# Allocating the buffers that TensorE reads first, each row on a multiple of 512 bytes

## The chip, the cores and the metric

The kernel runs on one core of a Trainium2 chip. A core has TensorE (PE in the profile; PEld is its loading of stationary operands), VectorE (DVE), ScalarE (ACT), GpSimd (POOL) and SyncE (SP, which here issues DMAs). The engines read their operands from SBUF, which has 128 partitions; a buffer takes the same range of byte addresses in each partition, so a buffer's place is one number, the address within a partition. TensorE writes its results to PSUM.

The metric is the time of one launch on the device, in microseconds (us), as the median of several runs. A profiled execution is one more launch, in which every instruction's start and duration is recorded.

## The reference, cut to what matters

Two sequences of 512 rows and 1024 channels go through the same trunk of two layers, and then a final RMSNorm. In each layer the normalised input is multiplied by one wide matrix; four attention mixers use its columns, each is gated and projected, and the merged sum goes through an output projection that is added to the input:

```python
def _layer(x, ...):
    xn = _rms_norm(x, norm_g)
    h = xn @ w_in
    h_a, h_b, h_c, h_d, z, mg = _split_cols(h, [A_IN, B_IN, C_IN, D_IN, GATE_IN, MERGE_IN])
    ys = [_mla_mixer(h_a, ...), _axial_gqa_mixer(h_b, ...), _sink_window_mixer(h_c, ...), _dilated_mixer(h_d, ...)]
    merged = jnp.zeros_like(x)
    for i in range(N_BRANCH):
        yi = ys[i] * jax.nn.silu(z[..., i * BRANCH_W:(i + 1) * BRANCH_W])
        gi = jax.nn.sigmoid(mg[..., i * D_MODEL:(i + 1) * D_MODEL])
        merged = merged + gi * (yi @ w_branch[i])
    return x + merged @ w_out
```

## The kernel before, in words

Everything is held with channels on the 128 partitions and the 512 rows of a sequence along the free dimension. The program makes four passes, layer by layer and within a layer sequence by sequence; each pass runs a list of steps (projections, attention heads, gates, merges), then the output projection, and prepares the next pass's normalised input. A scheduler of the tile framework sets the order of the instructions on each engine and puts in the semaphores.

**Products in three matmuls.** A float32 operand is split into a high part of type float32r and the rest, its low part. `mm3` (lines 121 to 124) makes one product from three matmuls: high weights by high data (L122), high weights by low data (L123), low weights by high data (L124). Each is 128x128 weights by 128x512 data. A matmul has a moving operand, which is streamed through the array column by column, and a stationary operand, the weights, which PEld loads ahead.

**The buffers that TensorE reads.** `xn0` to `xn7` hold the normalised input of a pass, high and low part as `[P, 2, 512]`; they are the moving operand of the wide projection (`project`, L126, and L656). `y` holds a gated mixer output in two parts, moving operand of the branch projections. `qk` holds queries, keys, latents and the merged sum, as moving and, for keys, as stationary operand. `ph` holds the two parts of the softmax weights (moving), `v` the values (stationary). `wh` and `wl` hold weight tiles of up to 640 columns, high and low part (stationary), made in `piece` (L99) from a tile `wr` that SP loads from DRAM: ScalarE copies the high part (L110), VectorE subtracts (L115), or the low part comes by DMA. Near the end of the last pass four of the `xn` buffers hold weight tiles of the output projection (`kept`), because their data is no longer needed.

**Where buffers lie.** All SBUF buffers come from one pool through `new(tag, shape, dt, bufs)`. A tag's buffers get their place where the tag is first asked for, one after the other from address 16,512 on; later requests for the tag turn over the same buffers. So the order of first requests is the order of addresses. In the kernel before this begins with the small constants (`ident`, `vecs`, `ones`, `heads`), goes on with the first pass's tiles, and a few tags of 64 or 240 bytes in between shift all that follows. A row of a `[P, 2, 512]` buffer is 4096 bytes, its two halves 2048 bytes each. The built program has these places (the last column is the address of the first buffer modulo 512; all buffers of the tag have the same):

| buffers | first to last start, before | modulo 512 |
|---|---|---|
| `s` (2 of 8192 bytes), `wr` (3 of 2560) | 18,432 to 39,936 | 0 |
| `wh`, `wl` (4 of 2560 each) | 42,496 to 60,416 | 0 |
| `qk` (8 of 4096) | 62,976 to 91,648 | 0 |
| `xn0` to `xn7` (4096 each) | 118,656 to 147,328 | 384 |
| `v` (4 of 2048) | 161,280 to 167,424 | 0 |
| `ph` (6 of 2048) | 187,904 to 198,144 | 0 |
| `y` (3 of 4096) | 200,320 to 208,512 | 128 |

Of the kernel before, what the change touches and what calls it, by code (L numbers as in the profile page):

```python
# [7 lines left out]
F32 = mybir.dt.float32  # L8
F32R = mybir.dt.float32r
# [4 lines left out]
P = 128  # L14
T = 512
DM = 1024
NK = DM // P
# [11 lines left out]
def trunk(ctx, tc, x0, x1, wp, wr, wu, wg, wb, wm, wo, vec, rope, msk, eye, y0, y1):  # L29
# [9 lines left out]
    def new(tag, shape, dt=F32, bufs=1):  # L39
        uid[0] += 1  # L40
        return sb.tile(shape, dt, tag=tag, name=f"{tag}_{uid[0]}", bufs=bufs)

    def bank(tag, bufs):
        uid[0] += 1
        return pp.tile([P, T], F32, tag=tag, name=f"{tag}_{uid[0]}", bufs=bufs)
# [15 lines left out]


    ident = new("ident", [P, P])
    vecs = new("vecs", [P, vec.shape[1]])

    def vcol(l, j):
        c = l * 24 + j
        return vecs[:, c : c + 1]

    ones = new("ones", [P, P])  # L70
    nc.vector.memset(ones, 1.0)
    heads = new("heads", [P, P])
# [462 lines left out]
    def begin(xin):  # L535

        nc.scalar.dma_start(out=vecs, in_=vec)
        warm = new("ms", [P, 16], F32, 2)
        act(out=warm, in_=ones[:, 0:16], func=AF.Exp)
        src = wp[0, T_D + 6 * 1]  # L540
        early = [new("s", [P, 4 * T], F32, 2) for _ in range(2)]
        xt = [early[k // 4][:, (k % 4) * T : (k % 4 + 1) * T] for k in range(NK)]
        xg, pieces, acc = [], [], None
        for k in range(NK):
            nc.sync.dma_start(out=xt[k], in_=xin[:, k, :])
            if k % 4 == 0:
                pieces.append(piece(src[k // 4], 512))
            x = new("qk", [P, 2, T], F32R, 8)
            act(out=x[:, 0, :], in_=xt[k], func=AF.Copy, scale=vcol(0, k))
            stt(out=x[:, 1, :], in0=xt[k], scalar=vcol(0, k), in1=f(x[:, 0, :]), op0=ALU.mult, op1=ALU.subtract)  # L550
            xg.append(x)
            acc = squares(acc, xt[k], k)
        load_tabs(("cos", "sin"))
        bc = rstd([acc], ones, DM, "lr")
        ct, st = new("u", [P, T], F32, 2), new("u", [P, T], F32, 2)
        xn = normalise(0, xt, bc, True)
        tt(out=ct, in0=tabs["cos"], in1=bc, op=ALU.mult)
        tt(out=st, in0=tabs["sin"], in1=bc, op=ALU.mult)
        return xn, (xg, pieces, ct, st, bc)
# [283 lines left out]
    xn, early = begin(x0)  # L843
    for n, args in enumerate(passes):
# [4 lines left out]
        xn = layer(*args, xn, ahead, early)  # L849
# [137 lines left out]
```

## Time and profile before

| | |
|---|---|
| median of 3 runs | 2187.64 us (2186.35 to 2188.82) |
| profiled execution, its own time | 2186.45 us |
| span from its first to its last instruction | 2184.7 us |
| granted TensorE clock, mean | 0.985 |
| TensorE matmuls | busy 2120.6 us (97%), 9550 |
| TensorE weight loads | busy 1722.1 us (79%), 9550 |
| VectorE | busy 1795.1 us (82%), 3113 |
| ScalarE | busy 1280.7 us (59%), 2167 |
| GpSimd | busy 411.2 us (19%), 145 |

A row of the groups names the line, the engine, the operation, the written and the read tiles (out<-in), the shape, the count, the busy time and the mean duration. A matmul's recorded duration includes its way through the array, and the next one starts before it ends; so consecutive matmuls are compared by the distance of their starts, which the timeline shows (start, duration, instruction, in us). In the rows of windows the first number is the window's length, then each engine's busy time with the count of instructions in brackets, the granted clock as a share of full speed, the DMA engines' busy share and GB/s.

### The profile page before, as it was taken

Reading aid. Unit: us, or ns where it says so; the run is one execution under the profiler, and the core shown is the slowest. Engines: PE = TensorE matmul, PEld = TensorE weight load, DVE = VectorE, ACT = ScalarE, POOL = GpSimd, SP = SyncE. Lnnn points to the kernel's source line nnn. Section 1 sums busy time; section 2 is a strip of 40 time slices with the busy share of each in tenths; the row PEclk is TensorE's granted clock in tenths of the full one; section 3 lists DMA queues with packets and bytes.
Section 4 is the critical chain, followed back from the end, with each engine's and each line's share of the span. In section 5 each row is a group of like instructions: output and inputs, shape, how many; then the busy total and the mean of one; then the engine's idle time right before and its main releaser. Section 6 shows DMA issues by size and latency. Waiting matters only on the chain.

```text
span 2184.7 us, 28862 instructions
## 1 busy us (share of the span) xinstructions
PE 2120.6 (97%) x9550; PEld 1722.1 (79%) x9550; DVE 1795.1 (82%) x3113; ACT 1280.7 (59%) x2167; POOL 411.2 (19%) x145
## 2 busy tenths in 40 slices
PE   7999999999999999999999998999899999999998
PEld 5887778878888778888888776888688887788887
DVE  8999999987478998785379999999866889997725
ACT  6746675444565767553366466754456757675434
POOL 0032313220013221220002222122200232122200
PEclk9999999999999999999999999999899999999999
DMA  6543444556754445556754434455466544455565
GB/s 213 169 145 120 141 141 163 175 186 210 240 165 145 139 138 159 162 191 212 245 179 155 139 117 134 156 166 177 161 226 223 152 152 135 145 158 164 179 207 185
DMA packets 189798, 369.76 MB, mean 169 GB/s; under 512 B 21328, under 2 KB 30032, under 8 KB 188880
## 3 DMA queue, kind: packets, MB, share of 16 engines
q1 hardware_dynamic: 181152, 351.11, 50.0%
q10 hardware_dynamic: 8496, 16.81, 2.3%
q8 instruction: 75, 1.23, 0.2%
q14 instruction: 75, 0.61, 0.1%
HBM read 273.99 MB, written 93.85 MB: 168 GB/s over the span
## 4 chain that ended last, share of the span: by engine, by line
PE 88%; DVE 8%; issue 1%; DMA 1%; ACT 1%; SPq 0%; DVEq 0%; ACTq 0%
PE mm L122 26%; PE mm L123 26%; PE mm L124 25%; PE so L343 1%; PE so L342 1%; PE ss L351 1%; DVE ph L140 1%; PE ss L352 1%; DMA s<-x 1%; DVE wl L115 1%; PE mi L268 1%; PE ss L124 1%; PE ss L123 1%; PE ss L447 1%; PE ss L122 1%
## 5 line engine op out<-in xcount | busy, mean ns | idle before, releaser
L123 PE MATMUL mm<-xn,wh 128*128 128x512 f32 x1992 | 788.5, 396 | 5.9 <-DVE xn L524 5.9
L122 PE MATMUL mm<-xn,wh 128*128 128x512 f32 x1992 | 791.3, 397 | 1.4 <-ACT xn L523 1.0
L124 PE MATMUL mm<-xn,wl 128*128 128x512 f32 x1992 | 788.7, 396 | 0.0
L110 ACT CAST wh<-wr 128x512 fp32r<-128x512 f32 (+1 forms) x596 | 387.1, 651 | 412.5 <-PE mm L123 302.0
L123 PEld LDWEIGHTS mm<-xn,wh 128*128 128x128 f32 x1992 | 376.3, 189 | 90.7 <-DVE xn L524 6.2
L122 PEld LDWEIGHTS mm<-xn,wh 128*128 128x128 f32 x1992 | 376.0, 189 | 88.8 <-ACT xn L523 1.4
L124 PEld LDWEIGHTS mm<-xn,wl 128*128 128x128 f32 x1992 | 376.1, 189 | 85.8 <-issue 1.0
L291 POOL PARTITION_ALL_REDUCE mr<-mr x64 | 239.2, 3737 | 512.2 <-DVE mr L347 265.8
L286 POOL PARTITION_ALL_REDUCE mr<-mr x64 | 129.8, 2029 | 985.3 <-DVE mr L470 577.5
L115 DVE TENSOR_TENSOR wl<-wr,wh 128x512 fp32r<-128x512 f32 (+2 forms) x304 | 247.2, 815 | 40.2 <-ACT wh L110 36.5
L140 DVE TENSOR_TENSOR ph<-s,ph 128x512 fp32r<-128x512 f32 (+2 forms) x256 | 184.9, 729 | 18.6 <-ACT ph L139 10.3
L139 ACT CAST ph<-s 128x512 fp32r<-128x512 f32 (+2 forms) x256 | 144.8, 577 | 30.6 <-PE so L490 11.0
L210 ACT COPY rs<-mm 32x512 f32<-32x512 f32 x240 | 138.8, 578 | 24.5 <-DVE rx L205 19.2
L713 DVE SCALAR_TENSOR_TENSOR th<-th,mm 128x512 f32<-128x512 f32 x96 | 65.4, 681 | 85.7 <-PE mm L124 83.5
L712 ACT ACTIVATE th<-mm 128x512 f32<-128x512 f32 x96 | 57.5, 599 | 132.2 <-PE mm L124 122.6
L122 PE MATMUL mm<-y,wh 128*128 128x512 f32 x256 | 105.1, 414 | 25.1 <-DVE mg L735 13.7
L122 PE MATMUL mm<-qk,wh 128*128 128x512 f32 (+1 forms) x328 | 122.4, 378 | 6.7 <-ACT wh L110 6.2
L124 PE MATMUL mm<-qk,wl 128*128 128x512 f32 (+1 forms) x328 | 122.3, 376 | 0.5 <-DVE wl L115 0.5
L123 PE MATMUL mm<-qk,wh 128*128 128x512 f32 (+1 forms) x328 | 122.3, 376 | 0.3 <-DVE qk L550 0.3
L124 PE MATMUL mm<-y,wl 128*128 128x512 f32 x256 | 104.4, 408 | 0.0
L123 PE MATMUL mm<-y,wh 128*128 128x512 f32 x256 | 104.1, 407 | 0.0
L327 ACT ACTIVATE s<-ss 128x512 f32<-128x512 f32 x128 | 72.3, 597 | 41.0 <-DVE ph L140 22.3
(182 smaller groups left out, 3247.3 us busy)
## 6 DMA issues: line engine op xcount, KB each, us to landing
wr<-wp SPq DMA_DIRECT2D x248, 256.0 KB, 2.8
wr<-wm SPq DMA_DIRECT2D x192, 320.0 KB, 3.2
lo_wp<-wl SPq DMA_DIRECT2D x124, 256.0 KB, 2.0
wl<-lo_wp SPq DMA_DIRECT2D x124, 256.0 KB, 2.7
lo_wm<-wl SPq DMA_DIRECT2D x96, 320.0 KB, 2.2
wl<-lo_wm SPq DMA_DIRECT2D x96, 320.0 KB, 2.9
wr<-wo SPq DMA_DIRECT2D x68, 256.0 KB, 3.6
wr<-wg SPq DMA_DIRECT2D x64, 256.0 KB, 2.8
```

The source lines that it names most:

```text
L110: nc.scalar.copy(out=hi[:, :n], in_=raw[:, :n])
L115: tt(out=lo[:, :n], in0=raw[:, :n], in1=f(hi[:, :n]), op=ALU.subtract)
L122: mm(ps, wh, xh, start=first, stop=False)
L123: mm(ps, wh, xl, start=False, stop=False)
L124: mm(ps, wl, xh, start=False, stop=last)
L139: nc.scalar.copy(out=hi, in_=src)
L140: tt(out=lo, in0=src, in1=f(hi), op=ALU.subtract)
L210: nc.scalar.copy(out=xs[c : c + 32], in_=ps[o : o + 32])
L286: nc.gpsimd.partition_all_reduce(m, t, P, RED.max)
L291: nc.gpsimd.partition_all_reduce(s, t, P, RED.add)
L327: act(out=s[:, j * T : (j + 1) * T], in_=ps, func=AF.Copy, scale=scale)
L713: stt(out=th, in0=th, scalar=1.0, in1=pb, op0=ALU.add, op1=ALU.mult)
```

## The change

Right after `new` is defined, a list of tags is asked for once each, in this order: `ms` and `rstd` (two and four buffers of 64 bytes), `xn0` to `xn7`, `qk`, `y`, `ph`, `v`, `wh`, `wl`. Nothing is written to the tiles of these requests. The six buffers of 64 bytes fill 384 bytes from 16,512 to 16,896, which is 33 times 512; each tag behind them has buffers of a whole multiple of 512 bytes.

```diff
     def new(tag, shape, dt=F32, bufs=1):
         uid[0] += 1
         return sb.tile(shape, dt, tag=tag, name=f"{tag}_{uid[0]}", bufs=bufs)
+
+
+    first = [("ms", [P, 16], F32, 2), ("rstd", [P, 16], F32, 4)]
+    first += [(f"xn{k}", [P, 2, T], F32R, 1) for k in range(NK)]
+    first += [("qk", [P, 2, T], F32R, 8), ("y", [P, 2, T], F32R, 3), ("ph", [P, T], F32R, 6), ("v", [P, 4, P], F32R, 4)]
+    first += [("wh", [P, 640], F32R, 4), ("wl", [P, 640], F32R, 4)]
+    for args in first:
+        new(*args)
```

The places in the changed program:

| buffers | first to last start, changed | modulo 512 |
|---|---|---|
| `xn0` to `xn7` | 16,896 to 45,568 | 0 |
| `qk` | 49,664 to 78,336 | 0 |
| `y` | 82,432 to 90,624 | 0 |
| `ph` | 94,720 to 104,960 | 0 |
| `v` | 107,008 to 113,152 | 0 |
| `wh`, `wl` | 115,200 to 133,120 | 0 |
| `s`, `wr` | 137,472 to 158,976 | 256 |
| `rx`, `rs`, `cos`, `sin` (VectorE and ScalarE) | 161,536 to 173,824 | 256 (0 before) |

The order of the instructions on every engine, their operands' shapes and the semaphores that each waits for are those of the kernel before; line numbers are 8 higher.

## The prediction

> **What bounds the kernel now.** I read the page first (busy shares, chain), then the groups by shape, then the timeline of TensorE for the distance between starts, then windows.
>
> ```profile
> span 2184.7 us, 28862 instructions
> PE 2120.6 (97%) x9550; PEld 1722.1 (79%) x9550; DVE 1795.1 (82%) x3113; ACT 1280.7 (59%) x2167; POOL 411.2 (19%) x145
> PE 88%; DVE 8%; issue 1%; DMA 1%; ACT 1%; SPq 0%; DVEq 0%; ACTq 0%
> L122 PE MATMUL mm<-xn,wh 128*128 128x512 f32 x1992 | 791.3, 397 | 1.4 <-ACT xn L523 1.0 <-DVE mg L735 0.4
> L122 PE MATMUL mm<-y,wh 128*128 128x512 f32 x256 | 105.1, 414 | 25.1 <-DVE mg L735 13.7 <-ACT y L139 11.4
> L122 PE MATMUL mm<-qk,wh 128*128 128x512 f32 x264 | 104.5, 401 | 6.7 <-ACT wh L110 6.2 <-DVE z L318 0.5
> L656 PE MATMUL mm<-xn,wh 128*128 128x512 f32 x64 | 16.8, 396 | 0.0
> ```
>
> TensorE sets the end: it is busy for 97% and is 88% of the chain that ended last. `mm3` issues three matmuls, so 3 x 1992 + 64 = 6040 matmuls of 512 columns stream `xn`, 3 x 256 = 768 stream `y`, and 3 x 264 = 792 stream `qk` through projections. The recorded durations (396 to 414 ns) overlap; what counts is the distance of starts. The timeline of TensorE has one stage where moving operands of the two kinds adjoin: the output projection of a pass (`qk`, rows on multiples of 512 bytes) and, with no gap, the first projections of the next pass (`xn`, 384 bytes past one).
>
> ```profile
> 522.17 0.39 PE L122 MATMUL mm<-qk,wh 128*128 128x512 f32 x1
> ...
> 565.52 0.39 PE L124 MATMUL mm<-qk,wl 128*128 128x512 f32 x1
> 565.75 0.40 PE L122 MATMUL mm<-xn,wh 128*128 128x512 f32 x1
> ...
> 590.01 0.40 PE L124 MATMUL mm<-xn,wl 128*128 128x512 f32 x1
> ```
>
> The output projection is 8 tiles of 24 matmuls, 192, so the first two rows are 191 steps apart: 43.35 us / 191 = 227.0 ns. The last two rows enclose 104 steps: 24.26 / 104 = 233.3 ns. Nothing is waited for in either, the weights come from the same `wh` and `wl`. The same difference stands elsewhere:
>
> ```profile
> 23.65 0.39 PE L124 MATMUL mm<-qk,wl 128*128 128x512 f32 x1
> ...
> 27.73 0.39 PE L124 MATMUL mm<-qk,wl 128*128 128x512 f32 x1
> 683.42 0.39 PE L124 MATMUL mm<-xn,wl 128*128 128x512 f32 x1
> ...
> 702.25 0.39 PE L124 MATMUL mm<-xn,wl 128*128 128x512 f32 x1
> 817.98 0.39 PE L122 MATMUL mm<-y,wh 128*128 128x512 f32 x1
> ...
> 821.92 0.40 PE L124 MATMUL mm<-y,wl 128*128 128x512 f32 x1
> ```
>
> The first pass projects its unnormalised input out of `qk` tiles with the weights that `xn` uses elsewhere: 18 steps in 4.08 us, 226.7 ns. A long `xn` run has 81 steps in 18.83 us, 232.5 ns. `y` (128 bytes past a multiple of 512) takes 17 steps in 3.94 us, 231.8 ns. So the slow kind is told by the moving operand's buffer, not by the stage or the weights. `xn` and `y` have two things in common that `qk` lacks: their rows are off a 512-byte multiple, and they lie above 118,000 in the partition. The change takes both away for both, so I need not know which of the two it is. I take 232.5 ns for the slow kind and 227.0 ns for the fast: 5.5 ns per matmul.
>
> **The change part by part.** It adds no instruction, removes none, and the order and the waits on every engine are the same; only addresses move. *Moving operands.* `xn` and `y` go to multiples of 512: (6040 + 768) x 5.5 ns = 37.4 us if all of it counts and all reach the fast spacing. Two deductions.
>
> First, stretches that VectorE paces. There TensorE already waits, and arriving sooner only lengthens the wait.
>
> ```profile
> core 0: us, PE busy (x) PEld busy (x) DVE busy (x) ACT busy (x) POOL busy (x), PEclk, DMA share, GB/s
> 130.00:290.00 160.00, 150.33 (x653) 117.04 (x652) 157.71 (x286) 95.75 (x161) 39.80 (x14) 0.98 0.42 135
> 1235.00:1365.00 130.00, 119.81 (x506) 92.74 (x505) 127.60 (x212) 81.69 (x136) 30.40 (x11) 0.95 0.39 125
> 490.00:770.00 280.00, 280.00 (x1285) 228.38 (x1284) 208.19 (x369) 163.93 (x277) 40.80 (x14) 1.00 0.57 180
> 815.00:1235.00 420.00, 420.00 (x1879) 343.68 (x1878) 310.05 (x541) 232.95 (x393) 64.85 (x24) 1.00 0.57 182
> ```
>
> In the first two windows VectorE is busy 98 to 99% and TensorE idles 10 us each. The counts of `xn` matmuls alone, in the same windows (and in two more of the later pass):
>
> ```profile
> 130.00:290.00 160.00, 97.05 (x398) 0.98 0.42 135
> 1235.00:1365.00 130.00, 71.45 (x284) 0.95 0.39 125
> 490.00:770.00 280.00, 193.31 (x796) 1.00 0.57 180
> 815.00:1235.00 420.00, 314.34 (x1264) 1.00 0.57 182
> 1568.00:1855.00 287.00, 199.80 (x823) 1.00 0.57 179
> 1895.00:2122.00 227.00, 179.82 (x706) 1.00 0.54 169
> ```
>
> I count the 682 `xn` matmuls of the first two windows as worth nothing: 3.8 us off. What is late next there is VectorE's own work, which the move leaves alone. 37.4 - 3.8 = 33.6 us.
>
> Second, restarts. A short run of the aligned kind does not start at 227:
>
> ```profile
> 710.55 0.40 PE L124 MATMUL mm<-qk,wl 128*128 128x512 f32 x1
> ...
> 712.86 0.39 PE L122 MATMUL mm<-qk,wh 128*128 128x512 f32 x1
> ...
> 714.00 0.39 PE L124 MATMUL mm<-qk,wl 128*128 128x512 f32 x1
> ```
>
> Ten steps take 2.31 us (231 ns each), the next five 1.14 us (228). After each interruption by a matmul of another shape some ten steps lose up to 4 ns of the gain, 40 ns. The interruptions can't be read from one row; bounds are none (0 us) and one for every ten of the 6808 (680 x 40 ns = 27 us). Most attention matmuls come in groups among long `xn` runs, so I take 160 of them, nearer the low end: 6.4 us. 33.6 - 6.4 is **27 us** of gain.
>
> *Weights.* `wh`, `wl` and `v` stay on multiples of 512 but `wh` and `wl` go from 42,496 up to 115,200. The trace has loads from a high, unaligned place: in the tail, `xn` buffers hold weights for matmuls of 256 columns.
>
> ```profile
> 2128.28 0.28 PE L123 MATMUL mm<-qk,wh 128*128 128x256 f32 x1
> ...
> 2128.76 0.28 PE L124 MATMUL mm<-qk,wl 128*128 128x256 f32 x1
> ...
> 2129.61 0.28 PE L122 MATMUL mm<-qk,xn 128*128 128x256 f32 x1
> ...
> 2130.20 0.28 PE L124 MATMUL mm<-qk,xn 128*128 128x256 f32 x1
> ```
>
> Four steps with `wh` take 0.48 us (120 ns), five with weights in `xn` 0.59 us (118). The place of the weights costs nothing there, even at half the matmul's length, so I take 0. Bounds: 2 ns either way on 9550 loads, 19 us, if a step of 512 columns showed what one of 256 does.
>
> *VectorE, ScalarE, DMA.* `s`, `wr`, `rx`, `rs`, `cos`, `sin` move from 0 to 256 past a multiple of 512.
>
> ```profile
> L524 DVE TENSOR_TENSOR xn<-s,xn x32: 682/684/693, 34.7 to 1602.5; 128x512 fp32r<-128x512 f32 x32
> L240 DVE TENSOR_TENSOR qk<-rx,qk x80: 684/687/2448, 47.5 to 1923.6; 64x512 fp32r<-64x512 f32 x80
> cos<-rope SPq DMA_DIRECT2D x1, 256.0 KB, 5.1
> bcos<-rope SPq DMA_DIRECT2D x1, 256.0 KB, 5.2
> ```
>
> The same subtraction has a median of 684 ns with `xn` at 384 and 687 with `qk` at 0; a table landing at 0 (`cos`) takes 5.1 us and one at 384 (`bcos`) 5.2. I take 0 for both. If VectorE gained or lost those 3 ns on each of its 3113 instructions, it would be 9 us of its time, most of it under TensorE's; the bound on the path is its 8% of the chain, under 1 us.
>
> **Two rules beside the rows.** The Trainium skill, page "SBUF — State Buffer", section "Operand start alignment", asks only that an operand start at a multiple of its element size and calls that legality, not speed; in its section on Door 1 the line that matters is 16 bytes, and both 384 and 128 are whole lines. By that page the two kinds of rows stream alike and the change is worth nothing, which is rival B below; the adjoining stretches at 227.0 and 233.3 ns disagree. The page "TensorE: Matmul & The Clock Gate", section "Wait — 56ns, not 53.3ns?", has 215.7 ns between warm 512-column matmuls; with it for the fast kind the sum would be an estimated 6808 x 16.8 ns = 114 us, but no long run here goes below 226.7.
>
> **The rivals.**
> A. *VectorE takes over more widely.* It is busy 82% of the span; where TensorE speeds up by 2.4%, VectorE's results may come no sooner, and the gain returns as waits at the next head. Then only the four windows above with VectorE under 80% (208 of 280, 310 of 420, and their like in the later layer) pay: 796 + 1264 + 823 + 706 = 3589 matmuls x 5.5 = 19.7 us, less the 6.4 for restarts: 13 us, about 2174. For: VectorE is 98% busy in two stretches. Against: the chain is 88% TensorE.
> B. *The address isn't the cause.* The 227 belongs to something else in those `qk` runs, or aligned rows settle only in long runs: no change, 2187.6. For: the short run's 231. Against: the step from 227.0 to 233.3 within one stage, and 226.7 with the `xn` projections' own weights at 23.65.
> C. *Height is the cause and counts for weights too* (slower). If what costs is a row above some address between 95,744 (the end of `qk`) and 115,200, `wh` and `wl` cross it: `xn` and `y` keep 232.5 and the 792 `qk` matmuls fall from 227.0 to 232.5: +4.4 us, 2192. It decides from the point where the stationary row's height is charged as the moving row's is. Against: 118 against 120 ns in the tail.
>
> **How the numbers follow.** The profiled execution took 2186.45 us, 1.2 below the median. Less 27 it is 2159.5, as a median about 2160. Chances: my forecast 0.61 (its own range 2146 to 2170: 41 us if neither deduction holds and attention's own matmuls, which stand among `xn`, add 4; 17 if restarts cost nearly three times what I took), A 0.23, B 0.11, C 0.05. The range 2146 to 2180 holds the forecast and A, and leaves out B and C, 16 in 100. A run of this kernel tells about 0.2% (4.4 us) from no change: faster 0.84, same 0.11, slower 0.05.
>
> **What would show it.** In the profile after: the 104 `xn` steps behind an output projection at 227 ns, in place of 233.3; TensorE's busy time down by some 25 us at the same count; waits of TensorE for `mg` L735 and `y` L139 (25 us before) grown by a few us, by more than 10 if A holds; VectorE's 684 ns and the DMA landings unchanged. If the `xn` steps stay at 232, B or C is right; C also lifts the `qk` steps. Wrong would be the whole argument if the steps fell to 227 and the time did not move.

## The result, and the profile after

The changed kernel takes 2164.33 us (median of 5, 2162.60 to 2165.96) against 2186.35 us for the kernel before, measured beside it (median of 5): 22.0 us less, a ratio of 0.9897, with a 95% interval of 0.9883 to 0.9912. The forecast was 2160, with a range of 2146 to 2180. The profiled execution took 2162.82 us, 23.6 less than the one before. One execution of this study, the profiled one of the kernel "Low, 256 past" below, ran at a granted clock of 0.75 and took 2599 us; it is left out of the times and ratios.

The page of the changed kernel (span, busy times, chain by engine), and two of its groups by shape; lines are 8 higher, L130 to L132 are `mm3`:

```profile
span 2161.0 us, 28862 instructions
PE 2087.6 (97%) x9550; PEld 1717.2 (79%) x9550; DVE 1793.6 (83%) x3113; ACT 1276.1 (59%) x2167; POOL 412.6 (19%) x145
PE 84%; DVE 11%; issue 2%; ACT 2%; DMA 1%; DVEq 0%; ACTq 0%; SPq 0%
L130 PE MATMUL mm<-xn,wh 128*128 128x512 f32 x1992 | 781.2, 392 | 2.9 <-ACT xn L531 2.3 <-DVE mg L743 0.6
L130 PE MATMUL mm<-y,wh 128*128 128x512 f32 x256 | 105.2, 415 | 26.3 <-DVE mg L743 14.2 <-ACT y L147 12.1
```

The span is 23.7 us shorter. TensorE's busy time fell by 33.0 us (2120.6 to 2087.6) at the same count, and its idle time grew by 9.3 us (64.1 to 73.4). VectorE's busy time hardly changed (1795.1 to 1793.6), but its share of the chain rose from 8% to 11%, as it would if it set the pace for longer. The recorded matmul durations are a poor guide to this: the mean of the `xn` row fell from 397 to 392 ns, that of the `y` row went from 414 to 415, though the steps of both became shorter. The starts tell it. TensorE's timeline at the same places as before, behind an output projection and in the run of `y`:

```profile
560.57 0.39 PE L132 MATMUL mm<-qk,wl 128*128 128x512 f32 x1
560.80 0.39 PE L130 MATMUL mm<-xn,wh 128*128 128x512 f32 x1
...
584.37 0.39 PE L132 MATMUL mm<-xn,wl 128*128 128x512 f32 x1
...
810.83 0.39 PE L130 MATMUL mm<-y,wh 128*128 128x512 f32 x1
...
814.71 0.39 PE L132 MATMUL mm<-y,wl 128*128 128x512 f32 x1
```

The 104 `xn` steps take 23.57 us, 226.6 ns each (233.3 before); the 17 `y` steps 228.2 ns (231.8 before).

The longest waits of TensorE in the changed kernel, and below them two of the kernel before that answer to its third and fourth row:

```profile
PE mm L130 <- DVE mg L743: 14.8, 10, 3.2
PE mm L130 <- ACT y L147: 12.1, 2, 7.6
...
PE so L351 <- DVE ph L148: 5.7, 8, 1.8
...
PE so L499 <- DVE ph L148: 4.3, 5, 2.3
```

```profile
PE so L343 <- DVE ph L140: 1.5, 2, 0.8
...
PE so L491 <- DVE ph L140: 1.4, 2, 0.9
```

The waits for `mg` and `y` hardly grew (14.1 and 11.4 before). In two of the attention's products of softmax weights and values, the waits for the low part of the softmax weights (`ph`, written by VectorE) grew by 7.1 us, most of the 9.3.

### The profile page after: what moved, and what is told of

Its sections match the earlier page's. It is cut to its first block, busy times and chain, and to the rows that moved or that the text cites. A ratio compares the mean times of both kernels' runs of the same rounds, so it can differ in the third digit from the quotient of the medians.

```text
span 2161.0 us, 28862 instructions
## 1 busy us (share of the span) xinstructions
PE 2087.6 (97%) x9550; PEld 1717.2 (79%) x9550; DVE 1793.6 (83%) x3113; ACT 1276.1 (59%) x2167; POOL 412.6 (19%) x145
## 4 chain that ended last, share of the span: by engine, by line
PE 84%; DVE 11%; issue 2%; ACT 2%; DMA 1%; DVEq 0%; ACTq 0%; SPq 0%
PE mm L130 24%; PE mm L131 24%; PE mm L132 24%; DVE wl L123 2%; DVE ph L148 1%; PE so L351 1%; PE so L350 1%; DMA s<-x 1%; PE ss L359 1%; PE ss L360 1%; PE mi L276 1%; PE ss L455 1%; PE mm L664 1%; PE ss L130 1%; PE ss L131 1%
## 5 line engine op out<-in xcount | busy, mean ns | idle before, releaser
L130 PE MATMUL mm<-xn,wh 128*128 128x512 f32 x1992 | 781.2, 392 | 2.9 <-ACT xn L531 2.3
L131 PE MATMUL mm<-xn,wh 128*128 128x512 f32 x1992 | 779.0, 391 | 4.5 <-DVE xn L532 4.5
L132 PE MATMUL mm<-xn,wl 128*128 128x512 f32 x1992 | 779.1, 391 | 0.0
L130 PEld LDWEIGHTS mm<-xn,wh 128*128 128x128 f32 x1992 | 374.8, 188 | 82.1 <-ACT xn L531 2.7
L132 PEld LDWEIGHTS mm<-xn,wl 128*128 128x128 f32 x1992 | 374.8, 188 | 77.5 <-issue 1.0
L130 PE MATMUL mm<-y,wh 128*128 128x512 f32 x256 | 105.2, 415 | 26.3 <-DVE mg L743 14.2
L130 PE MATMUL mm<-qk,wh 128*128 128x512 f32 (+1 forms) x328 | 120.9, 374 | 7.2 <-ACT wh L118 6.1
L132 PE MATMUL mm<-qk,wl 128*128 128x512 f32 (+1 forms) x328 | 121.2, 372 | 0.7 <-DVE wl L123 0.7
L132 PE MATMUL mm<-y,wl 128*128 128x512 f32 x256 | 103.3, 404 | 0.0
```

What stands on the lines that cost most here:

```text
L130: mm(ps, wh, xh, start=first, stop=False)
L131: mm(ps, wh, xl, start=False, stop=False)
L132: mm(ps, wl, xh, start=False, stop=last)
```

## The experiments

Four questions: is it the row's start or its height; a multiple of what; does the weights' place count; and where did the 9.3 us go. In the kernels that differ in places alone, the order of TensorE's 9550 matmuls is that of the kernel before.

**Stretches of matmuls alone.** A kernel with nothing but stretches of 48 matmuls, weights turning over four slices of one buffer:

```diff
+    def stretch(b, m, w, n=48, cols=T):
+        ps = pp.tile([P, T], F32, tag=f"b{b % 8}", name=f"b_{b}", bufs=1)
+        for i in range(n):
+            s = slice((i % 4) * P, (i % 4 + 1) * P)
+            nc.tensor.matmul(ps[:, :cols], w[:, s], m[:, :cols], start=i == 0, stop=i == n - 1)
...
```

> All of the trunk is left out: the kernel only runs 21 stretches of 48 matmuls (128x128 weights, 512 moving columns of float32r) and copies its input to its output. Each stretch streams one buffer whose row starts 0, 32, 64, 128, 192, 256, 384 or 448 bytes past a multiple of 512 at a low address (19,456 to 34,240) or 0, 128, 256 past one at a high address (142,848 to 147,200); the last stretches move the weights instead (0, 128, 256 past, low and high). Theory 'row start': 227 ns between starts wherever the moving row starts on a multiple of 512, low or high, and 231 to 234 ns for 128 and 384; the weights' place changes nothing. Which of 32, 64, 192, 256, 448 are slow it leaves open. Rival 'height': 227 ns for every low row, 232 for every high one. Rival 'weights count too': the stretches with moved weights are slow as well.

The timeline merges each stretch into a row, so the difference of two rows' first numbers, divided by 48, is the step. `m128x` is a low moving row 128 bytes past a multiple of 512, `h` a high one; `w` and `k` are low and high weights.

```profile
70.07 11.32 PE L70 MATMUL b<-m128x,w0x 128*128 128x512 f32 x48
81.22 11.36 PE L70 MATMUL b<-m192x,w0x 128*128 128x512 f32 x48
92.42 11.09 PE L70 MATMUL b<-m256x,w0x 128*128 128x512 f32 x48
103.34 11.35 PE L70 MATMUL b<-m384x,w0x 128*128 128x512 f32 x48
...
125.72 11.06 PE L70 MATMUL b<-h0x,w0x 128*128 128x512 f32 x48
136.62 11.36 PE L70 MATMUL b<-h128x,w0x 128*128 128x512 f32 x48
147.82 11.06 PE L70 MATMUL b<-h256x,w0x 128*128 128x512 f32 x48
158.71 11.05 PE L70 MATMUL b<-m0x,w0x 128*128 128x512 f32 x48
169.60 11.32 PE L70 MATMUL b<-m0x,w128x 128*128 128x512 f32 x48
180.75 11.05 PE L70 MATMUL b<-m0x,w256x 128*128 128x512 f32 x48
191.64 11.05 PE L70 MATMUL b<-m0x,k0x 128*128 128x512 f32 x48
202.52 11.32 PE L70 MATMUL b<-m0x,k128x 128*128 128x512 f32 x48
213.68 11.09 PE L70 MATMUL b<-m128x,w128x 128*128 128x512 f32 x48
224.61 11.05 PE L70 MATMUL b<-m128x,k128x 128*128 128x512 f32 x48
235.49 11.05 PE L70 MATMUL b<-m0x,w0x 128*128 128x512 f32 x48
```

Height is out: the high row at 0 takes (136.62 - 125.72) / 48 = 227.1 ns, the high one at 128 233.3. A multiple of 512 is more than is needed: 256 past takes 227.5 ns low and 226.9 high. The weights count too, as one rival had it: moved by 128 under an unmoved row they cost the same as a moved row (232.3 ns; high weights 232.5), moved by 256 nothing. What no expectation foresaw is that with *both* 128 past the step is back at 227.7 and 226.7. So the theory "row start" falls as it was put. What fits all the rows is the distance of the moving row's start from the weights' start, modulo 256.

**The distance in fine steps.**

> All of the trunk is left out, as in the first run of stretches. Here the weights stay at one place (w0, a multiple of 256) and the moving row's start is swept 0, 4, 8, 16, 32, 48, ... 240, 252 bytes past a multiple of 256; four last stretches have 256 and 128 columns with weights 128 bytes off and not off. Theory 'distance': what counts is the distance of the moving row's start from the weights' start modulo 256; 226.7 ns at 0, 228 to 234 ns at 32, 64, 128 and 192 as in the first run; 16, 48, 80 and the like also between 228 and 234; at 4, 8 and 252 it leaves open whether a few bytes already cost. At 256 columns it expects 120 against 118 to 119 ns or no difference, since the tail of the kernel showed none. Rival 'row start of each': the same numbers here, told apart by the kernel in which everything lies 128 past. If any distance gave less than 226.7 ns, a faster placing than the changed one would exist.

Weights at one place, the moving row's start swept (a buffer's name is its distance in bytes); the last rows have 256 and 128 columns:

```profile
46.32 11.52 PE L62 MATMUL b<-m4x,w0x 128*128 128x512 f32 x48
57.68 11.35 PE L62 MATMUL b<-m8x,w0x 128*128 128x512 f32 x48
...
102.38 11.15 PE L62 MATMUL b<-m64x,w0x 128*128 128x512 f32 x48
113.37 11.26 PE L62 MATMUL b<-m80x,w0x 128*128 128x512 f32 x48
...
214.02 11.36 PE L62 MATMUL b<-m224x,w0x 128*128 128x512 f32 x48
225.22 11.05 PE L62 MATMUL b<-m240x,w0x 128*128 128x512 f32 x48
236.10 11.05 PE L62 MATMUL b<-m252x,w0x 128*128 128x512 f32 x48
247.00 5.92 PE L62 MATMUL b<-m0x,w128x 128*128 128x256 f32 x48
252.75 5.92 PE L62 MATMUL b<-m0x,w0x 128*128 128x256 f32 x48
258.51 5.47 PE L62 MATMUL b<-m0x,w128x 128*128 128x128 f32 x48
```

Four bytes past the weights' phase cost most, 236.7 ns; 64 past 229.0; all others from 8 to 224 between 231 and 235. Four and 16 bytes *ahead* of it (252 and 240) cost nothing: 227.1 and 226.7. Distance 0 takes 226.7 in the first stretches (202.52 - 191.64, in 48 steps). No distance tried gives less, so none of these placings beats distance 0. At 256 columns, 128 off and not off take 119.8 and 120.0 ns: at this distance the cost that stands at 512 columns is absent at 256.

**Aligned, but high.** The order of before, but those small buffers that shifted `xn` and `y` are put last (the list is cut):

```diff
+    first = [("ident", ...), ("vecs", ...), ("ones", ...), ("heads", ...), ("ms", ...)]
+    first += [("s", ...), ("wr", ...), ("wh", ...), ("wl", ...), ("qk", ...)]
+    first += [("rx", ...), ("rs", ...), ("cos", ...), ("sin", ...), ("lr", ...), ("u", ...)]
+    first += [(f"xn{k}", [P, 2, T], F32R, 1) for k in range(NK)]
+    first += [("bcos", ...), ("bsin", ...), ("atab", ...), ("band", ...), ("tri", ...), ("band4", ...)]
+    first += [("v", ...), ("th", ...), ("z", ...), ("mr", ...), ("yf", ...), ("ph", ...), ("y", ...)]
+    for args in first:
+        new(*args)
```

> The buffers keep the order and the height that they had before (xn from 118,272, ph from 187,392, y from 199,680), but the small buffers are put at the end, so that every row that TensorE reads starts on a multiple of 512. Theory 'row start': xn and y steps fall to 227 to 228 ns as in the changed kernel, time 2164 (2160 to 2168). Rival 'height': xn and y steps stay at 232.5, time 2186 (2182 to 2190).

2167.92 us, ratio 0.991 (0.989 to 0.993). The 104 `xn` steps behind the output projection, in its timeline:

```profile
563.65 0.39 PE L131 MATMUL mm<-xn,wh 128*128 128x512 f32 x1
...
587.23 0.39 PE L133 MATMUL mm<-xn,wl 128*128 128x512 f32 x1
```

226.7 ns each, with `xn` 384 bytes below its old place: the steps of the change without its "low". The time is 19.3 us less than that of the kernel before beside it, where the change gave 22.0; the intervals overlap.

**Low, but 128 past.** `xn` and `y` ahead of the small buffers:

```diff
+    first = []
+    first += [(f"xn{k}", [P, 2, T], F32R, 1) for k in range(NK)] + [("y", [P, 2, T], F32R, 3)]
+    first += [("ms", [P, 16], F32, 2), ("rstd", [P, 16], F32, 4)]
+    first += [("qk", [P, 2, T], F32R, 8), ("ph", [P, T], F32R, 6), ("v", [P, 4, P], F32R, 4)]
+    first += [("wh", [P, 640], F32R, 4), ("wl", [P, 640], F32R, 4)]
+    for args in first:
+        new(*args)
```

> The buffers that TensorE reads lie first and low as in the changed kernel, but xn and y come ahead of the small ones, so their rows start 128 bytes past a multiple of 512 (xn from 16,512, y from 49,280); qk, ph, v, wh, wl stay on multiples. Theory 'row start': xn and y steps 232 to 233 ns, time 2186 (2182 to 2190). Rival 'height': 227 to 228, time 2164.

2186.30 us, ratio 0.9998 (0.9989 to 1.0008): no gain. Its timeline, the same 104 steps at 233.3 ns:

```profile
568.41 0.40 PE L130 MATMUL mm<-xn,wh 128*128 128x512 f32 x1
...
592.67 0.40 PE L132 MATMUL mm<-xn,wl 128*128 128x512 f32 x1
```

**Low, 256 past.** The same with `ms` ahead of `xn` and `rstd` behind `y`:

```diff
-    first = []
+    first = [("ms", [P, 16], F32, 2)]
...
-    first += [("ms", [P, 16], F32, 2), ("rstd", [P, 16], F32, 4)]
+    first += [("rstd", [P, 16], F32, 4)]
```

> As the kernel with xn and y 128 past, but 256 bytes past a multiple of 512 (xn from 16,640, y from 49,408). If a multiple of 512 is what matters: xn and y steps 231 to 233 ns, 2183 to 2188. If a multiple of 256 (or less) is enough: 227 to 228 ns, 2160 to 2168. Rival 'height': 2164 as well, so this run alone doesn't tell the second from the third; the kernel at 128 does.

2167.26 us, ratio 0.991 (0.9893 to 0.9928): a multiple of 256 is enough in the kernel too. This rests on the times; no timeline of it is read.

**Everything 128 past.** The change's list without `ms` and `rstd` at its head, so that none of the buffers in the list starts on a multiple of 256:

```diff
-    first = [("ms", [P, 16], F32, 2), ("rstd", [P, 16], F32, 4)]
-    first += [(f"xn{k}", [P, 2, T], F32R, 1) for k in range(NK)]
+    first = [(f"xn{k}", [P, 2, T], F32R, 1) for k in range(NK)]
```

> The same list of first requests without the six small buffers at its head: xn, qk, y, ph, v, wh and wl all start 128 bytes past a multiple of 512 (xn from 16,512, wh from 114,816), none on a multiple of 256. Theory 'distance' (moving row from weights, modulo 256): all distances are 0, steps 227 to 228 ns for xn, y and qk, time 2164 to 2168. Rival 'row start of each': xn and y at 232.5 and qk too, time 2186 to 2192.

2166.78 us, ratio 0.9912 (0.9897 to 0.9928). The 104 steps in its timeline, 226.6 ns:

```profile
562.08 0.39 PE L128 MATMUL mm<-xn,wh 128*128 128x512 f32 x1
...
585.65 0.39 PE L130 MATMUL mm<-xn,wl 128*128 128x512 f32 x1
```

The gain stands though none of these buffers starts on a multiple of 256. The distance counts, not the starts.

**Only the weights moved.** The changed kernel with 128 bytes ahead of `wh`:

```diff
-    first += [("wh", [P, 640], F32R, 4), ("wl", [P, 640], F32R, 4)]
+    first += [("nw", [P, 16], F32, 2), ("wh", [P, 640], F32R, 4), ("wl", [P, 640], F32R, 4)]
```

> The changed kernel with one small buffer (nw, 128 bytes) put ahead of wh and wl, so that the weights start 128 bytes past a multiple of 512 (from 115,328) while xn, qk, y, ph and v stay on multiples. Theory 'distance': the projections out of xn, y and qk are all 128 away from their weights; steps 232 to 233 ns for each; the time goes back past the kernel before, by 792 qk matmuls at 5.5 ns, 4 us: 2186 to 2192. Rival 'the moving rows alone': steps stay 227 to 228, 2164.

2190.31 us, ratio 1.002 (1.0011 to 1.003): slower than before, as expected. The output projection's 191 `qk` steps and the 104 `xn` steps behind it, in its timeline:

```profile
524.94 0.40 PE L130 MATMUL mm<-qk,wh 128*128 128x512 f32 x1
...
569.34 0.39 PE L132 MATMUL mm<-qk,wl 128*128 128x512 f32 x1
569.57 0.39 PE L130 MATMUL mm<-xn,wh 128*128 128x512 f32 x1
...
593.74 0.40 PE L132 MATMUL mm<-xn,wl 128*128 128x512 f32 x1
```

They are at 232.5 and 232.4 ns now; `qk` was at 227.0 before. Moving the two tags by 128 bytes undoes all of the change and takes the fast `qk` steps too, 26 us against the changed kernel. (What lies behind `wh` and `wl` moves by 128 bytes as well; these projections read none of it.)

**The missing gain, as a pair.** VectorE's work is cut in the same way in a kernel with the old places and in one with the new ones:

```diff
     def piece(src, n, into=None):
...
-        if into is None:
-            hi = new("wh", [P, 640], F32R, 4)
-            lo = new("wl", [P, 640], F32R, 4)
-        else:
-            hi, lo = into[:, 0, :], into[:, 1, :]
+        hi = new("wh", [P, 640], F32R, 4) if into is None else into[:, 0, :]
         nc.scalar.copy(out=hi[:, :n], in_=raw[:, :n])
-        key = (src.tensor.name, src.offset)
-        if key in lows:
-            nc.sync.dma_start(out=f(lo[:, :n]), in_=lows.pop(key))
-            return hi, lo
-        tt(out=lo[:, :n], in0=raw[:, :n], in1=f(hi[:, :n]), op=ALU.subtract)
...
-        return hi, lo
+        return hi, hi
...
     def halves(w):
         n = w.shape[-1]
         hi = new("ph", [P, T], F32R, 6)
-        lo = new("ph", [P, T], F32R, 6)
-        split(hi[:, :n], lo[:, :n], w)
-        return hi[:, :n], lo[:, :n]
+        nc.scalar.copy(out=hi[:, :n], in_=w)
+        return hi[:, :n], hi[:, :n]
```

> Places as in the kernel before (xn 384 and y 128 off, weights on multiples of 512), but VectorE's work is cut: the low parts of the weights and of the softmax weights are left out (their subtractions, and the weights' way through DRAM); TensorE runs the same matmuls with the high part in their place, so the result is less exact. It is one half of a pair. VectorE loses about 430 us of its 1795. Theory 'VectorE took the missing gain': TensorE's waits shrink to a third, the time falls to 2110 to 2150. Rival: no such fall, 2170 to 2187.

> The other half of the pair: the same cut of VectorE's work with the places of the changed kernel. Theory 'VectorE took the missing gain': with nothing to wait for, the move is worth what the steps of TensorE say, 30 to 35 us less than the first half of the pair. Rival 'the gain is lost elsewhere (restarts, DMA)': the difference stays at 22 us or less.

2123.22 us with the old places, 2089.06 with the new: a difference of 34.2 us, where the full kernels differ by 22.0. The pages, old places and new:

```profile
span 2121.9 us, 26607 instructions
...
PE 2095.9 (99%) x9550; PEld 1711.9 (81%) x9550; DVE 1464.3 (69%) x2553; ACT 1281.7 (60%) x2167; POOL 379.6 (18%) x145
```

```profile
span 2087.3 us, 26607 instructions
...
PE 2059.6 (99%) x9550; PEld 1708.8 (82%) x9550; DVE 1461.2 (70%) x2553; ACT 1280.9 (61%) x2167; POOL 379.0 (18%) x145
```

VectorE has 331 us less than in the full kernel (I had expected 430). TensorE's busy time falls by 36.3 us between the two, and its idle time grows by only 1.7 (26.0 to 27.7), against 9.3 in the full kernels. TensorE's waits for `mg`, for `y` and for VectorE's `ph`, most of its waiting in the full kernels, are gone in both halves. With less for VectorE to do, nearly all that TensorE's steps save reaches the end. The cut also takes away DMAs of the low weight parts and changes the scheduler's order, in both halves alike; whether these have a part in it was not tried apart.

**Some of VectorE's work on GpSimd.** In the changed kernel, every third subtraction:

```diff
-        tt(out=lo[:, :n], in0=raw[:, :n], in1=f(hi[:, :n]), op=ALU.subtract)
+        sub = nc.gpsimd.tensor_tensor if len(lows) % 3 == 2 else tt
+        sub(out=lo[:, :n], in0=raw[:, :n], in1=f(hi[:, :n]), op=ALU.subtract)
```

> The changed kernel with every third subtraction of a weight's low part (about 100 of 304) moved from VectorE to GpSimd, which is busy 19%. Theory 'VectorE sets the pace in the attention stretches of the first sequence': 100 x 0.8 us less on VectorE; of the 12 us by which TensorE's waits grew some come back, 2150 to 2162. Rival: GpSimd's own work (the reductions over partitions that the softmax waits for) is delayed by the subtractions queued ahead of it, or its switch between the two kinds of work costs, and the time rises, 2166 to 2200. I lean to the rival, 60 to 40.

2517.74 us, ratio 1.1514 (1.1494 to 1.1533). TensorE's longest wait in it, and the moved subtractions among GpSimd's groups:

```profile
PE mm L133 <- POOL wl L124: 111.2, 31, 11.2
...
L124 POOL TENSOR_TENSOR wl<-wr,wh 128x512 fp32r<-128x512 f32 (+2 forms) x101 | 164.6, 1630 | 778.2 <-ACT wh L118 233.1 <-issue 134.5 <-DMA x<-mg 83.2
```

The time goes the rival's way, far beyond its numbers (2166 to 2200), but its mechanism is not shown. The 101 subtractions take a mean of 1630 ns on GpSimd, over three shapes; all 304 took a mean of 813 on VectorE in the changed kernel. GpSimd is idle for 778 us in all just before them, 233.1 of it until `wh` is there. TensorE waits 111.2 us, in 31 times, for the moved low parts themselves, which neither the theory nor the rival had named; its idle time is 329.2 us in all, its busy time 2187.2 at a granted clock of 0.926. How much comes from the order in GpSimd's queue, which the softmax's reductions share, and how much from a switch between the two kinds of work was not separated. No version that keeps all of the work beats the changed kernel.

## Why the prediction was right, and where it was not

**The sign, the size and the place** came out: 2164 against 2160, from the steps of `xn` and `y`. That step rested on the starts in five stretches of one trace, the longest of them adjoining in one stage, and it held to half a nanosecond in the `xn` steps there (forecast 227.0, measured 226.6).

**"I need not know which of the two it is"** (off a multiple of 512, or high) was enough for the forecast only by luck, and wrong as a list of causes. It was neither: the height is out by the aligned, high kernel (0.991), and the multiple of 512 by the kernel with everything 128 past (0.9912). The cause is the distance between the moving row's start and the weights' start, modulo 256. In the kernel before `wh` and `wl` lay at 0, `xn` 384 and `y` 128 past, both 128 off; `qk` was 0 off. The change works because its moving and its stationary buffers get the same phase, not because the phase is zero. The forecast never weighed that; with the weights 128 bytes further the same reasoning would have met 2190.

**The weights at cost 0** was the step whose reasoning failed. The row that I took, 256-column matmuls with weights in `xn`, showed no cost because at 256 columns there is none (119.8 and 120.0 ns in the stretches); carried to 512 columns it misled. Moving only the weights costs 26 us, more than the 19 given as its bound. The step came out at 0 by luck: the change also leaves the weights on multiples of 512. Rival C, that weights count too, was right that the stationary row takes part. Its sum for `xn`, `y` and `qk` all slow, 2192, is what the kernel with moved weights shows, 2190; but it had the wrong coordinate, height for phase.

**Restarts, 6.4 us.** TensorE's busy time fell by 33.0 us, against 37.4 - 6.4 = 31.0 from these terms (the list of signs says some 25). The fast steps settled at 226.7 and not 227.0, which is worth 2 us on 6808 steps. The term itself had the right size by luck. In the changed kernel's trace, runs of `xn` or `y` steps less than 300 ns apart begin 733 times, not 160; the steps of a run start at 230 ns (`xn`) and reach 226.7 after some ten, as I had read it; but most runs are short, and a restart costs 8 ns in the mean, not 40. Together that is 5.7 us. The stretches show it too: the first ten steps with both rows 128 past, behind a slow stretch, took a mean of 231.6 ns, which is why their row came to 227.7. What sets the ten steps stays open.

**Stretches that VectorE paces, 3.8 us: the mis-sized term.** TensorE's idle time grew by 9.3. I counted only the two windows in which VectorE was over 98% busy. The same matmuls in the changed kernel:

```profile
127.90:288.70 160.80, 147.91 (x653) 115.60 (x652) 157.09 (x285) 95.92 (x161) 40.56 (x15) 0.99 0.41 134
1220.50:1349.70 129.20, 117.75 (x506) 92.99 (x505) 126.33 (x212) 81.68 (x137) 30.73 (x11) 0.95 0.39 127
```

There TensorE idles 24.3 us, where it had idled 19.9, so 4.5 are lost, near the 3.8, and the two windows together are no shorter: as forecast, the move is worth nothing in them. The other half of the 9.3, some 5 us, was lost outside them, where the sum had nothing; part of that, too, are waits for `ph`. The waits that I named for a check, `mg` and `y`, barely moved. Rival A, with all stretches but four lost (13 us of gain), was too dark. The pair with less VectorE work supports the reason: there the difference is 34.2 us.

**VectorE, ScalarE and DMA at 0** held: VectorE's busy time is 1793.6 us after 1795.1 and ScalarE's 1276.1 after 1280.7, with `s`, `wr`, `rx` and `rs` 256 past a multiple of 512 and not on one. The `wr` tiles loaded from `wp` land in 2.8 us in both.

**The two rules.** The Trainium skill's page "SBUF — State Buffer", section "Operand start alignment", asks for a multiple of the element size and says that this is about legality, not speed. That the change would then be worth nothing was my reading of it, and the runs disagree: four bytes of distance, a whole element, cost 10 ns of a 512-column step. By the 215.7 ns of the Trainium skill's page "TensorE: Matmul & The Clock Gate", section "Wait — 56ns, not 53.3ns?", the steps should have gone lower; no distance here went below 226.7 with float32r, and no run shows why.

## What to carry to other kernels

Where TensorE sets the time, compare the distances of its starts by operand, not the recorded durations: here 5.5 ns per 512-column float32r step was worth 1%, and the durations hid it. Before the change the mean of the fast `qk` row was 401 ns and that of the slow `xn` row 397. In such a kernel give the moving and the stationary buffers the same start modulo 256, which the order of allocation alone can do, and look again after any small buffer is put ahead of one of them. Then take off a TensorE saving what the engine that feeds it will not follow: here 9.3 of 33.0 us came back as waits, half of them outside the stretches in which that engine looked full.

## What the runs showed of the hardware that was not expected

The step of TensorE depends on the distance in a partition between the streamed row and the weights, neither of which matters alone: 227 ns per 512-column float32r step at a distance of 0, 240 or 252 bytes modulo 256 (226.7 in the settled runs), 236.7 at 4, 229 at 64, 231 to 235 at the other distances tried; at 256 columns no cost at a distance of 128. A collision of the streamed row with the weights that are loaded beside it would fit, but no run here shows where the time goes. Other data types, row lengths between 256 and 512, and other distances at 256 columns were not tried.
